# A hybrid decoder layer: attention's value products in float32r parts, heads in turn on two PSUM banks

## The chip, the cores and the metric

The kernel runs on one core of one Trainium2 chip. The metric is the device time of one execution in microseconds. TensorE (PE) multiplies matrices, VectorE (DVE) and ScalarE (ACT) work on rows of 128 partitions and also read PSUM, GpSimd (POOL) works in SBUF only, and SyncE (SP) issues the loads.

## The reference

One layer for 512 tokens of 1024 features, in float32. A normalised input goes through one projection; its columns feed three mixers, which are joined, projected by w_out and added to the input; a squared-ReLU MLP follows. The mixer that matters here is the sparse attention with 6 heads of 64 features on 2 key/value heads. For each head there are three softmaxes over keys: over 31 compressed blocks, over the selected blocks, and over a window. With 512 tokens the 16 selected blocks and the window of 512 hold every earlier key, so two of the three are plain causal attention with their own keys and values:

```python
p_c = masked_softmax(s, cmp_end[None, :] <= pos[:, None])
o_c = jnp.einsum('bhgqc,bhcd->bhgqd', p_c, vc)
...
o_s = jnp.einsum('bhgqn,bhqnd->bhgqd', masked_softmax(s, mask_s), vsel)
...
o_w = jnp.einsum('bhgqk,bhkd->bhgqd', masked_softmax(s, mask_w), vwb)
return gb[..., 0:1] * o_c + gb[..., 1:2] * o_s + gb[..., 2:3] * o_w
```

The other mixers are a gated delta rule (a chunked recurrence with 6 heads) and a causal pooling.

## The kernel before, in words

The kernel is written in a tile framework: the program gives instructions in an order, the framework puts each on its engine's queue by a schedule that it works out beforehand, and each queue then runs in order. A PSUM bank or a buffer of a pool is handed on in the order of the program; who asks for it waits until the last reader of the holder before is done.

Most large products are done in float32r parts: a value is cast to a high part (ACT) and the difference is the low part (DVE or GpSimd), and `mm3` (L142) issues high x high, high x low and low x high. `split_rows` (L147) makes both parts from PSUM. Some products stay in float32, which PE issues as two records each.

Up to about 252 us the input projection runs in slabs. Of these `vcopy` (L683) copies the attention's values for the four token blocks into `Vt`, `prep_heads` (L526) makes the queries and keys `XT`, and `compress_half` (L583) makes the compressed keys `KCT` and values `VC`. Beside them the delta rule's solves and its scan (`gdn_step`, L868) run on banks of their own; the scan's products use bank 3 (`ps_`), and after its nine steps `gdn_out` (L913) normalises each token block and transposes it through bank 3 (`go`) into chunks 0 to 2 of `yTh` and `yTl`.

The attention stage is `attentions` (L1140), walked in turn with `out_gdn` (L1210) by `side_by_side` (L936). Heads go in pairs. For each pair a bank 7 is taken as accumulator (`pa`), and for each of two branches and each head of the pair:

- `probs` (L1092): for each block i of 128 queries the scores against (i + 1) x 128 keys (L1100, L1101, float32r, and the mask L1102), their maximum (DVE), the exponential with its sum (ACT), and the scaling by gate over sum, blocks 0 to 2 on DVE and block 3 on ACT (L1113, L1115).
- `values` (L1117): the ten blocks of 128x128 probabilities are transposed in three groups (`BLKS`): four blocks with key block 0, three with key block 1 and one with key block 3, two with key block 2. Each group is copied from PSUM (first and third on ACT, second on DVE) and multiplied in float32 with 64 columns of values (L1135), the first head of a pair into rows 0 to 63 of the accumulator, the second into rows 64 to 127. The groups have 512, 384 + 128, and 256 columns.

The compressed branch (`cmp_probs`, L1056) gives transposed probabilities of three heads at once, and L1155 multiplies 32 rows of them per head with `VC`. `finish` (L1162) splits the pair's accumulator into one chunk of `yTh` and `yTl` (chunks 3 to 5).

`out_gdn` loads w_out by chunks of 128 rows (`load_w`, L1173: raw load on SP, high part on ACT, low part on DVE) into ten slots in two pools, and adds y times w_out to the residual in three passes (`out_tile`, L1196): chunks 6 and 7, then 0 to 2, and after the attention 3 to 5. The norm and the MLP follow.

Of the kernel before, what the change touches and what calls it, by code (L numbers as in the profile page):

```python
# [26 lines left out]
H = 6  # L27
# [10 lines left out]
def trunk_kernel(ctx, tc, x, norm_mix, w_in, conv_w, a_log, dt_bias, gdn_norm, nsa_q_norm, nsa_k_norm,  # L38
# [14 lines left out]
    def nm(s):  # L53
        _n[0] += 1
        return f"{s}{_n[0]}"
# [19 lines left out]


    r2 = ctx.enter_context(pool("r2", 1))
    N2 = 25

    def t2(shape, name, dt=F32):  # L80
        return r2.tile(shape, dt, tag="t", name=nm(name), bufs=N2)
# [308 lines left out]
    halves = [slice(0, 64), slice(64, 128)]  # L390

    XT, Vt = {}, {}
    VC = ctile([96, 2, HD], F32, "VC")
    KCT = ctile([P, 2, 64], F32R, "KCT")
    kr = gdp.tile([P, NT, H, HD], F32, tag="kr", name="kr")
    qr = gdp.tile([P, NT, H, HD], F32, tag="qr", name="qr")
# [186 lines left out]
    def compress_half(a, q):  # L583
        if q == 0:
            cst_[a] = pc_(), flat[a]
        acc, fs = cst_[a]
        for j in range(8 * q, 8 * q + 8):
            r0 = P * j
            with tc.issue_after(slabs2.ins):
                hi, lo = load_half([(0, cmp_w1[0, a, r0:r0 + P, :])], "c", (4, 2, 1), "AV")  # L590
            for n_, w in enumerate((hi, lo)):
                PE.matmul(acc[:, 0:256], fs[j // 4][:, j % 4, :], w[:, 0, :], start=(j == 0 and n_ == 0),  # L592
                          stop=(j == 15 and n_ == 1))
            yield 0.21
        if q == 0:
            return
        w2 = cmp_.tile([P, 2, HD], F32, tag="w2", name=nm("w2"))
        S.dma_start(w2, cmp_w2[0, a].rearrange("(m p) d -> p m d", p=P))
        hid = cmp_.tile([P, 256], F32, tag="hid", name=nm("hid"))
        S.copy(hid, acc[:, 0:256])  # L600
        hp_ = acc[:, 256:384]
        for m in range(2):
            PE.matmul(hp_[:, ts(m, 64)], hid[:, ts(m, P)], id2, start=True, stop=True)
        hh = cmp_.tile([P, 128], F32, tag="hh", name=nm("hh"))
        ht = cmp_.tile([P, 128], F32, tag="ht", name=nm("ht"))
        S.activation(ht, hp_[:, 0:128], AF.Tanh, scale=0.5)
        S.mul(hh, hp_[:, 0:128], 0.5)
        V.scalar_tensor_tensor(hh, ht, 1.0, hh, ALU.add, ALU.mult)
        if a == 0:
            kp = acc[:, 384:448]  # L610
            for m in range(2):
                PE.matmul(kp[0:64, 0:HD], hh[:, ts(m, 64)], w2[:, m, :], start=(m == 0), stop=(m == 1))
            kcs = cmp_.tile([64, HD], F32, tag="kcs", name=nm("kcs"))
            ss = sml.tile([P, 1], F32, tag="ss1", name=nm("ss"))
            r = sml.tile([P, 1], F32, tag="r1", name=nm("r"))
            S.activation(kcs, kp[0:64, 0:HD], AF.Square, accum_out=ss[0:64])
            V.tensor_scalar(ss[0:64], ss[0:64], 0.5 / HD, 0.5 * EPS, ALU.mult, ALU.add)
            rsqrt(r[0:64], ss[0:64], 1, 64)
            V.scalar_tensor_tensor(kcs, kp[0:64, 0:HD], r[0:64], gk_b[0:64, 0, :], ALU.mult, ALU.mult)
            kx = cmp_.tile([64, 2, P], F32, tag="hid", name=nm("kx"))  # L620
            S.copy(kx[:, 0, 0:HD].bitcast(F32R), kcs)
            S.copy(kx[:, 0, HD:P].bitcast(F32R), kcs)
            V.tensor_tensor(kx[:, 1, 0:HD], kcs, kx[:, 0, 0:HD], ALU.subtract)
            V.tensor_tensor(kx[:, 1, HD:P], kcs, kx[:, 0, 0:HD], ALU.subtract)
            kq = acc[:, 0:128]
            for b in range(2):
                PE.transpose(kq[:, ts(b, 64)], kx[:, b, :], ident[:64, :64])
            S.copy(KCT.rearrange("p k (b n) -> p b k n", b=2), kq[:, 0:128].rearrange("p (b k n) -> p b k n", b=2, k=2))
        else:
            vp = acc[:, 384:512]  # L630
            for rep in range(3):
                for kv in range(2):
                    for m in range(2):
                        PE.matmul(vp[32 * rep:32 * rep + 32, ts(kv, HD)], hh[:, 64 * m + 32 * kv:64 * m + 32 * kv + 32],
                                  w2[:, m, :], start=(m == 0), stop=(m == 1))
            S.copy(VC, vp[0:96, 0:128].rearrange("p (k d) -> p k d", k=2))


    PW = ctile([P, 2, P], F32, "PW")
# [41 lines left out]
                G.tensor_tensor(z3, z3, gnh.unsqueeze(1).to_broadcast([P, n // HD, HD]), ALU.mult)  # L681

    def vcopy(b0, pss):  # L683
        for b in range(2):
            if b not in Vt:
                Vt[b] = t2([P, 2, 4, HD], "Vt")
            S.copy(Vt[b][:, :, b0:b0 + 2, :], pss[b][:, :, 0:128].rearrange("p i (k d) -> p i k d", k=2))

    def conv_slab(cols):
        fs = {"q": 0, "k": 384, "v": 768, "u": 2718}  # L690
# [354 lines left out]
    wr = ctx.enter_context(pool("wr", 2, side="right"))  # L1045
    nwe = ExitStack()
    nw = nwe.enter_context(pool("nw", 2, side="right"))
    wop = [nwe.enter_context(pool(f"wo{n}", n, side="right")) for n in (4, 6)]
    gd.close()
    fe = ExitStack()  # L1050
    wq = fe.enter_context(pool("wq", 2))


    pn, pt_, pa = banks(0, 1), banks(2, 6), banks(7)

    def cmp_probs(kv):  # L1056

# [25 lines left out]
        tp = pt_()  # L1083
        for i in range(NT):
            PE.transpose(tp[0:96, ts(i, P)], pc[:, i].rearrange("p g n -> p (g n)"), ident)
        pt = nw.tile([96, T], F32, tag=f"pcT{kv}", bufs=1, name=nm("pcT"))
        S.copy(pt, tp[0:96])
        return pt

    BLKS = ([(0, i) for i in range(4)], [(1, i) for i in range(1, 4)] + [(3, 3)], [(2, 2), (2, 3)])  # L1090
# [1 line left out]
    def probs(h, br, out):  # L1092

        kv = h // 3
        kb = 6 + 4 * br + 2 * kv
        sm = sml.tile([P, NT], F32, tag="sm4", bufs=4, name=nm("sm"))
        for i in range(NT):
            n = (i + 1) * P
            sc = pn()
            PE.matmul(sc[:, 0:n], XT[h][:, ts(i, P)], XT[kb][:, 0:n], start=True, stop=False)  # L1100
            PE.matmul(sc[:, 0:n], XT[h][:, ts(i, P)], XT[kb + 1][:, 0:n], start=False, stop=False)  # L1101
            PE.matmul(sc[:, n - P:n], identb, negb, start=False, stop=True)  # L1102
            mx = sml.tile([P, 1], F32, tag="mx", bufs=4, name=nm("mx"))
            V.tensor_reduce(mx, sc[:, 0:n], AX.X, ALU.max, negate=True)
            p_ = nw.tile([P, n], F32, tag=f"P{i}", name=nm("P"))
            S.activation(p_, sc[:, 0:n], AF.Exp, bias=mx, accum_out=sm[:, i:i + 1])
            out.append(p_)
            yield 0.11 * (i + 1)
        V.reciprocal(sm, sm)
        V.tensor_tensor(sm, sm, gate[:, :, 3 * h + 1 + br], ALU.mult)  # L1110
        for i in range(NT):
            if i == 3:
                S.mul(out[i], out[i], sm[:, i:i + 1])  # L1113
            else:
                V.tensor_scalar(out[i], out[i], sm[:, i:i + 1], None, ALU.mult)  # L1115

    def values(acc, h, br, Ps):  # L1117

        a = h % 2
        for b, blks in enumerate(BLKS):  # L1120
            n = len(blks) * P
            tp = pt_()
            for c, (k, i) in enumerate(blks):
                PE.transpose(tp[:, ts(c, P)], Ps[i][:, ts(k, P)], ident)  # L1124
            pt = nw.tile([P, n], F32, tag=f"pt{b}", name=nm("pt"))
            if b == 1:
                V.tensor_copy(pt, tp[:, :n])
            else:
                S.copy(pt, tp[:, :n])
            yield 0.4  # L1130
            c = 0
            while c < len(blks):
                k, i = blks[c]
                m = sum(1 for x_ in blks if x_[0] == k)
                PE.matmul(acc[halves[a], i * P:(i + m) * P], Vt[k // 2][:, k % 2, 2 * br + h // 3, :],  # L1135
                          pt[:, c * P:(c + m) * P], start=False, stop=(br == 1 and k == 2), skip_group_check=True)
                c += m
            yield 0.4

    def attentions():  # L1140
        last = iter(())
        for pr in range(3):
            hd = (2 * pr, 2 * pr + 1)
            for h in hd:
                if h % 3 == 0:
                    pcT[h // 3] = cmp_probs(h // 3)
            acc = pa()
            for br in range(2):
                for h in hd:
                    Ps = []  # L1150
                    yield from in_turn((probs(h, br, Ps), last))
                    if br == 0 and h == hd[0]:
                        for a, h_ in enumerate(hd):
                            r = slice(32 * (h_ % 3), 32 * (h_ % 3) + 32)
                            PE.matmul(acc[halves[a]], VC[r, h_ // 3], pcT[h_ // 3][r], start=True, stop=False,  # L1155
                                      skip_group_check=True)
                    last = values(acc, h, br, Ps)
                    if br == 1 and h == hd[1]:
                        last = finish(last, pr, acc)
        yield from last  # L1160

    def finish(gen, pr, acc):  # L1162
        yield from gen
        y_tiles((3 + pr,))
        split_rows(yTh[3 + pr], yTl[3 + pr], acc)
        have.add(("y", 3 + pr))

    pcT = {}


    wo = {}
# [11 lines left out]

    def load_wo(*cs):
        for c in cs:
            wo[c] = load_w(wop[c < 4], w_out[0, ts(c, P), :].unsqueeze(1), "wo", "AV")

    w1s = []
    PASS = [(6,7),(0,1,2),(3,4,5)]
# [215 lines left out]
```

## Time and profile before

| | |
|---|---|
| median of three runs | 734.46 us (734.19 to 738.3) |
| the profiled execution | 738.01 us |
| its span, first to last instruction | 736.0 us |
| mean granted clock of TensorE | 0.986 |

The profile is one execution, taken with the hardware profiler. Its span is 2.0 us shorter than its time. An instruction's duration is not the time that it adds on PE: matmuls overlap, and the start of the next tells how long one holds the engine. The chain of waits is the chain of work that ended last, followed back, and its pieces add up without overlap.

### The profile page before, as it was taken

To read this page: it belongs to the slowest core of one execution; us is meant where nothing else is said; L and a number is where in the kernel's file an instruction comes from. 1 tells how busy PE (TensorE), PEld (TensorE's weight loads), DVE (VectorE), ACT (ScalarE), POOL (GpSimd) and SP (SyncE) were. 2 spreads that over 40 slices of the span, in tenths; PEclk is the share of its full clock that TensorE was granted. 3 is DMA by queue.
4 is the path that set the end of the run, shared out by engine and by line. 5 is a ranking of instruction groups with operands and counts; after the bars stand their busy time and mean duration, and the time that the engine had idled before them with its cause. 6 is when DMAs were issued, how large, how long until landed. Compare 5 with 4: busy or idle time off the path is not lost.

```text
span 736.0 us, 13221 instructions
## 1 busy us (share of the span) xinstructions
PE 707.9 (96%) x5147; PEld 566.7 (77%) x5147; DVE 550.3 (75%) x1010; ACT 369.6 (50%) x728; POOL 214.4 (29%) x292
## 2 busy tenths in 40 slices
PE   8999978999999899999999999999999999999997
PEld 6888766788889766665568987888888888888885
DVE  5776997688786596866545799796868587796836
ACT  5455834456673364555534745444553454445440
POOL 5734355350614410000010150504123050504123
PEclk9999988999999999999999999999999999999999
DMA  6243222124221251013002142514142332412103
GB/s 218 65 116 85 73 50 66 31 65 115 74 59 31 86 209 51 29 58 115 0 1 87 53 166 64 177 30 144 56 154 75 115 114 77 152 36 80 57 1 114
DMA packets 49779, 61.67 MB, mean 84 GB/s; under 512 B 5479, under 2 KB 42549, under 8 KB 49718
## 3 DMA queue, kind: packets, MB, share of 16 engines
q1 hardware_dynamic: 48852, 60.64, 26.2%
q8 instruction: 40, 0.66, 0.4%
q10 hardware_dynamic: 866, 0.20, 0.1%
q14 instruction: 21, 0.17, 0.1%
HBM read 58.73 MB, written 2.10 MB: 83 GB/s over the span
## 4 chain that ended last, share of the span: by engine, by line
PE 63%; DVE 7%; ACT 2%; issue 1%; DMA 0%; POOL 0%; ACTq 0%; DVEq 0%; POOLq 0%
PE ps L143 16%; PE ps L145 16%; PE ps L144 16%; PE ps L1135 4%; PE ps L429 3%; PE ps L1124 2%; PE ps L800 1%; PE ps L1100 1%; PE ps L1101 1%; PE ps L905 1%; DVE x L1374 1%; PE ps L592 1%; DVE bl L1281 1%; DMA raw<-in_w_out_dram 0%; PE ps L1247 0%
## 5 line engine op out<-in xcount | busy, mean ns | idle before, releaser
L145 PE MATMUL ps<-h2h,lw 128*128 128x512 f32 (+1 forms) x280 | 104.9, 376 | 0.0
L144 PE MATMUL ps<-h2l,hw 128*128 128x512 f32 (+1 forms) x280 | 104.4, 374 | 0.1
L143 PE MATMUL ps<-h2h,hw 128*128 128x512 f32 (+1 forms) x280 | 103.8, 374 | 0.0
L1288 POOL TENSOR_TENSOR al<-gF,ah 128x512 fp32r<-128x512 f32 x24 | 34.7, 1446 | 230.0 <-ACT ah L1287 191.0
L143 PE MATMUL ps<-bh,ah 128*128 128x512 f32 x224 | 88.5, 395 | 0.6 <-DVE x L1374 0.6
L144 PE MATMUL ps<-bl,ah 128*128 128x512 f32 x224 | 88.2, 394 | 0.0
L145 PE MATMUL ps<-bh,al 128*128 128x512 f32 x224 | 84.7, 394 | 0.0
L1374 DVE TENSOR_TENSOR x<-ps,x 128x512 f32<-128x512 f32 x112 | 73.0, 682 | 14.2 <-PE ps L145 14.1
L1281 DVE TENSOR_TENSOR bl<-w2r,bh 128x1024 fp32r<-128x1024 f32 x40 | 57.8, 1447 | 7.2 <-ACT bh L1280 7.2
L135 POOL TENSOR_TENSOR lo<-raw,hi 128x512 fp32r<-128x512 f32 (+1 forms) x36 | 48.1, 1351 | 50.2 <-ACT hi L134 50.0
L144 PEld LDWEIGHTS ps<-h2l,hw 128*128 128x128 f32 x280 | 52.6, 188 | 10.6 <-DVE h2l L1252 0.3
L145 PEld LDWEIGHTS ps<-h2h,lw 128*128 128x128 f32 x280 | 52.5, 188 | 10.0
L143 PEld LDWEIGHTS ps<-h2h,hw 128*128 128x128 f32 x280 | 52.3, 188 | 9.7
L1288 POOL TENSOR_TENSOR al<-gS,ah 128x512 fp32r<-128x512 f32 x32 | 54.0, 1705 | 17.3 <-ACT ah L1287 17.3
L1280 ACT CAST bh<-w2r 128x1024 fp32r<-128x1024 f32 x40 | 41.8, 1048 | 32.1 <-PE ps L145 31.9
L134 ACT CAST hi<-raw 128x512 fp32r<-128x512 f32 (+1 forms) x76 | 36.9, 517 | 33.2 <-DMA raw<-in_w_in_dram 14.5
L143 PEld LDWEIGHTS ps<-bh,ah 128*128 128x128 f32 x224 | 42.1, 188 | 11.2 <-ACT ah L1287 0.8
L145 PEld LDWEIGHTS ps<-bh,al 128*128 128x128 f32 x224 | 42.1, 188 | 9.9
L144 PEld LDWEIGHTS ps<-bl,ah 128*128 128x128 f32 x224 | 42.1, 188 | 9.7
L135 DVE TENSOR_TENSOR lw<-raw,hw 128x1024 fp32r<-128x1024 f32 x32 | 39.1, 1254 | 9.6 <-ACT hw L134 9.4
L134 ACT CAST hw<-raw 128x1024 fp32r<-128x1024 f32 x32 | 32.2, 1047 | 26.4 <-PE ps L144 23.4
L144 PE MATMUL ps<-hTl,hi 128*128 128x512 f32 x104 | 43.6, 420 | 0.0
(365 smaller groups left out, 1691.0 us busy)
## 6 DMA issues: line engine op xcount, KB each, us to landing
raw<-in_w_ffn_dram SPq DMA_DIRECT2D x32, 512.0 KB, 3.7
w2r<-in_w_ffn_dram SPq DMA_DIRECT2D x32, 512.0 KB, 4.5
raw<-in_w_in_dram SPq DMA_DIRECT2D x24, 256.0 KB, 2.8
raw<-in_w_in_dram SPq DMA_DIRECT2D x36, 128.0 KB, 2.4
x<-in_x_dram SPq DMA_DIRECT2D x8, 512.0 KB, 5.7
raw<-in_cmp_w_dram SPq DMA_DIRECT2D x32, 128.0 KB, 2.2
raw<-in_w_out_dram SPq DMA_DIRECT2D x8, 512.0 KB, 4.1
out_dram<-x SPq DMA_DIRECT2D x8, 256.0 KB, 2.0
```

The costliest lines, as they stand in the source:

```text
L134: {"A": S.copy, "V": V.tensor_copy, "G": G.tensor_copy}[e[0]](hi[:, k], r)
L135: {"V": V, "G": G}[e[1]].tensor_tensor(lo[:, k], r, f32v(hi[:, k]), ALU.subtract)
L143: PE.matmul(ps, ah, bh, start=start, stop=False, **kw)
L144: PE.matmul(ps, ah, bl, start=False, stop=False, **kw)
L145: PE.matmul(ps, al, bh, start=False, stop=stop, **kw)
L429: PE.matmul(ps[:, ts(i, 256)], a_[:, k, ts(2 * b + i, P)], w_, start=(k == 0 and n_ == 0 and i == 0), stop=(k == KC - 1 and n_ == 2 and i ...
L1124: PE.transpose(tp[:, ts(c, P)], Ps[i][:, ts(k, P)], ident)
L1135: PE.matmul(acc[halves[a], i * P:(i + m) * P], Vt[k // 2][:, k % 2, 2 * br + h // 3, :], pt[:, c * P:(c + m) * P], start=False, stop=(br = ...
L1280: S.copy(hi, src)
L1281: V.tensor_tensor(lo, src, f32v(hi), ALU.subtract)
L1288: G.tensor_tensor(lo, src, f32v(hi), ALU.subtract)
L1374: V.tensor_tensor(x2[i][:, cs], acc[bk, t_], x2[i][:, cs], ALU.add)
```

## The change

- The value tiles `Vt` are one per token block; for blocks 0, 1 and 3 they hold [high | low] float32r parts side by side, 128 columns. Block 2 stays float32.
- In `values` the first two groups' transposed probabilities become high and low float32r parts (a cast on ACT, a subtraction on DVE), and each is multiplied with the 128 columns, so rows 0 to 63 of the accumulator hold the products with high values and rows 64 to 127 those with low ones. The third group stays as it was and goes to rows 0 to 63, and its copy stays on ACT.
- One accumulator belongs to one head and not to a pair. Heads go one after the other, both branches of each, on banks 7 and 3 in turn.
- The compressed values become [high | low] parts, zero outside a head's 32 rows (`VCz`), the compressed probabilities high and low parts, and each head has two float32r matmuls.
- `finish` runs for each head: ACT copies the low-value rows, DVE adds the others, and after each second head the chunk is split as before.
- Block 2's probabilities are scaled on ACT, as block 3's are.
- w_out's low parts are computed on GpSimd. The pool of six w_out slots is opened after the delta rule's pools are closed, and the common pool has 27 buffers for 25.

```diff
-    N2 = 25
+    N2 = 27
...
-    VC = ctile([96, 2, HD], F32, "VC")
+    VC = ctile([96, 2, 2, HD], F32R, "VC")
...
-            S.copy(VC, vp[0:96, 0:128].rearrange("p (k d) -> p k d", k=2))
+            split_rows(VC[:, :, 0], VC[:, :, 1], vp[0:96, 0:128].rearrange("p (k d) -> p k d", k=2))
...
     def vcopy(b0, pss):
-        for b in range(2):
-            if b not in Vt:
-                Vt[b] = t2([P, 2, 4, HD], "Vt")
-            S.copy(Vt[b][:, :, b0:b0 + 2, :], pss[b][:, :, 0:128].rearrange("p i (k d) -> p i k d", k=2))
+        for i in range(NT):
+            src = pss[i // 2][:, i % 2, 0:128].rearrange("p (k d) -> p k d", k=2)
+            if i not in Vt:
+                Vt[i] = t2([P, 4, HD], "Vt") if i == 2 else t2([P, 4, 2, HD], "Vt", F32R)
+            if i == 2:
+                S.copy(Vt[i][:, b0:b0 + 2], src)
+            else:
+                split_rows(Vt[i][:, b0:b0 + 2, 0], Vt[i][:, b0:b0 + 2, 1], src)
...
-    wop = [nwe.enter_context(pool(f"wo{n}", n, side="right")) for n in (4, 6)]
+    wop = [nwe.enter_context(pool("wo4", 4, side="right"))]
     gd.close()
+    wop.append(nwe.enter_context(pool("wo6", 6, side="right")))
...
-    pn, pt_, pa = banks(0, 1), banks(2, 6), banks(7)
+    pn, pt_, pa = banks(0, 1), banks(2, 6), banks(7, 3)
...
-        pt = nw.tile([96, T], F32, tag=f"pcT{kv}", bufs=1, name=nm("pcT"))
-        S.copy(pt, tp[0:96])
+        pt = [nw.tile([96, T], F32R, tag=f"pcT{c}{kv}", bufs=1, name=nm("pcT")) for c in "hl"]
+        split_rows(pt[0], pt[1], tp[0:96])
...
-            if i == 3:
+            if i >= 2:
                 S.mul(out[i], out[i], sm[:, i:i + 1])
...
-            pt = nw.tile([P, n], F32, tag=f"pt{b}", name=nm("pt"))
-            if b == 1:
-                V.tensor_copy(pt, tp[:, :n])
+            if b == 2:
+                pt = [nw.tile([P, n], F32, tag=f"pt{b}", name=nm("pt"))]
+                S.copy(pt[0], tp[:, :n])
             else:
-                S.copy(pt, tp[:, :n])
+                pt = [nw.tile([P, n], F32R, tag=f"pt{c}{b}", name=nm("pt")) for c in "hl"]
+                split_rows(pt[0], pt[1], tp[:, :n])
...
-                PE.matmul(acc[halves[a], i * P:(i + m) * P], Vt[k // 2][:, k % 2, 2 * br + h // 3, :],
-                          pt[:, c * P:(c + m) * P], start=False, stop=(br == 1 and k == 2), skip_group_check=True)
+                for p_ in pt:
+                    v_ = Vt[k][:, 2 * br + h // 3]
+                    PE.matmul(acc[0:64 if b == 2 else P, i * P:(i + m) * P],
+                              v_ if b == 2 else v_.rearrange("p c d -> p (c d)"),
+                              p_[:, c * P:(c + m) * P], start=False, stop=(br == 1 and b == 2), skip_group_check=True)
...
     def attentions():
+        G.memset(f32v(VCz), 0.0)
+        for h in range(H):
+            r = slice(32 * (h % 3), 32 * (h % 3) + 32)
+            S.copy(VCz[r, h], f32v(VC[r, h // 3]).rearrange("p c d -> p (c d)"))
         last = iter(())
-        for pr in range(3):
-            hd = (2 * pr, 2 * pr + 1)
-            for h in hd:
-                if h % 3 == 0:
-                    pcT[h // 3] = cmp_probs(h // 3)
+        for h in range(H):
+            if h % 3 == 0:
+                pcT[h // 3] = cmp_probs(h // 3)
             acc = pa()
             for br in range(2):
-                for h in hd:
-                    Ps = []
-                    yield from in_turn((probs(h, br, Ps), last))
...
+                Ps = []
+                yield from in_turn((probs(h, br, Ps), last))
+                if br == 0:
+                    for n_, p_ in enumerate(pcT[h // 3]):
+                        PE.matmul(acc, VCz[:, h], p_, start=n_ == 0, stop=False, skip_group_check=True)
+                last = values(acc, h, br, Ps)
+            last = finish(last, h, acc)
         yield from last
...
-    def finish(gen, pr, acc):
+    def finish(gen, h, acc):
         yield from gen
...
+        a = halves[h % 2]
+        if h % 2 == 0:
+            os_[0] = nw.tile([P, T], F32, tag="o", bufs=1, name=nm("o"))
+        o = os_[0]
+        S.copy(o[a], acc[halves[1 - h % 2]])
+        V.tensor_tensor(o[a], acc[a], o[a], ALU.add)
+        if h % 2:
+            y_tiles((3 + h // 2,))
+            split_rows(yTh[3 + h // 2], yTl[3 + h // 2], o)
+            have.add(("y", 3 + h // 2))
...
-            wo[c] = load_w(wop[c < 4], w_out[0, ts(c, P), :].unsqueeze(1), "wo", "AV")
+            wo[c] = load_w(wop[c < 4], w_out[0, ts(c, P), :].unsqueeze(1), "wo", "AG")
```

## Rows read from the trace of the kernel before

**Rows 1.** The page: busy time, share of the span and instructions of each engine.

```profile
PE 707.9 (96%) x5147; PEld 566.7 (77%) x5147; DVE 550.3 (75%) x1010; ACT 369.6 (50%) x728; POOL 214.4 (29%) x292
```

**Rows 2.** Busy time of each engine in three stretches of the attention stage.

```profile
core 0: us, PE busy (x) PEld busy (x) DVE busy (x) ACT busy (x) POOL busy (x), PEclk, DMA share, GB/s
252.00:293.00 41.00, 39.77 (x344) 27.25 (x343) 33.48 (x86) 22.36 (x54) 6.54 (x8) 1.00 0.43 155
293.00:318.00 25.00, 23.97 (x125) 16.25 (x126) 19.08 (x63) 13.18 (x38) 1.19 (x1) 1.00 0.07 22
318.00:373.60 55.60, 53.95 (x264) 30.88 (x264) 33.53 (x80) 31.19 (x83) 0.00 (x0) 1.00 0.18 58
```

**Rows 3.** The chain of waits from 318 to 374 us, its shares by line.

```profile
by line: PE ps L1135 35.6%; PE ps L1124 14.6%; PE ps L1100 9.2%; PE ps L143 7.5%; PE ps L145 6.6%; PE ps L144 6.2%; PE ps L1101 5.9%; PE ps L1155 3.6%; PE ps L1102 2.6%; ACT pt L1129 2.1%; ACT P L1106 1.9%; DVE mx L1104 1.7%; DVE P L1115 1.
```

**Rows 4.** The chain, pieces of values in float32: start us, us, what.

```profile
288.36 0.58 PE ps L1135 x2
...
290.75 1.00 PE ps L1135 x2
...
324.06 1.00 PE ps L1155 x4
...
372.11 1.44 PE ps L1135 x6
```

**Rows 5.** The chain, pieces in float32r of 384, 512 and 128 columns.

```profile
290.50 0.18 PE ps L1101
...
318.23 0.23 PE ps L143
...
319.20 0.11 PE ps L1101
```

**Rows 6.** Groups of ACT by form: busy us, mean ns of one, idle before.

```profile
L1113 ACT ACTIVATE P<-P,sm 128x512 f32<-128x512 f32 x12 | 8.6, 720 | 4.1 <-DVE sm L1110 2.9 <-DVE P L1115 0.8 <-DVE rs L111 0.5
...
L1129 ACT COPY pt<-ps 128x512 f32<-128x512 f32 x12 | 7.0, 585 | 14.0 <-PE ps L1124 13.8
...
L1106 ACT ACTIVATE P<-ps,mx 128x384 f32<-128x384 f32 x12 | 7.0, 583 | 5.5 <-DVE mx L1104 5.3 <-PE ps L1124 0.2
```

**Rows 7.** Groups of DVE by form.

```profile
L135 DVE TENSOR_TENSOR lwo<-raw,hwo 128x1024 fp32r<-128x1024 f32 x8 | 9.9, 1237 | 1.0 <-ACT hwo L134 1.0
...
L1127 DVE COPY pt<-ps 128x512 f32<-128x512 f32 x12 | 8.2, 686 | 3.2 <-PE ps L1124 3.1
...
L1115 DVE TENSOR_SCALAR P<-P,sm 128x384 f32<-128x384 f32 x12 | 5.0, 415 | 0.0
```

**Rows 8.** Groups of POOL by form, low parts of 512 and 256 columns.

```profile
L135 POOL TENSOR_TENSOR lo<-raw,hi 128x512 fp32r<-128x512 f32 x32 | 44.0, 1393 | 41.4 <-ACT hi L134 41.2
...
L135 POOL TENSOR_TENSOR lo<-raw,hi 128x256 fp32r<-128x256 f32 x4 | 4.0, 1020 | 8.8 <-ACT hi L134 8.8
```

**Rows 9.** Timeline, DVE's L1110 alone and beside a POOL operation: start us, us.

```profile
297.73 0.16 DVE L1110 TENSOR_TENSOR sm<-sm,gate 128x4 f32<-128x4 f32 x1
...
306.20 1.19 POOL L924 TENSOR_TENSOR vb<-vb,zt 128x384 f32<-128x384 f32 x1 [25.32 <-DVE vb L923]
...
306.64 0.77 DVE L1110 TENSOR_TENSOR sm<-sm,gate 128x4 f32<-128x4 f32 x1
```

**Rows 10.** Timeline: a w_out cast, the scan's last product, the outputs through bank 3.

```profile
264.81 1.04 ACT L134 CAST hwo<-raw 128x1024 fp32r<-128x1024 f32 x1
...
292.44 0.51 PE L905 MATMUL ps<-vn,QK 64*64 64x64 f32 x6
...
295.05 0.55 PE L927 MATMUL ps<-ident,vb 128*128 128x128 f32 x3
...
318.47 0.28 DVE L149 TENSOR_TENSOR yTl<-ps,yTh 128x128 fp32r<-128x128 f32 x1
```

**Rows 11.** Timeline: the split of the last pair of heads.

```profile
373.59 0.59 ACT L148 CAST yTh<-ps 128x512 fp32r<-128x512 f32 x1 [1.07 <-PE ps L1135]
...
374.21 0.69 DVE L149 TENSOR_TENSOR yTl<-ps,yTh 128x512 fp32r<-128x512 f32 x1 [3.16 <-ACT yTh L148]
```

More of the change, by code (lines that the diff above doesn't have):

```diff
@@ L1117, in values @@
     def values(acc, h, br, Ps):
-        a = h % 2
         for b, blks in enumerate(BLKS):
@@ L1140, in attentions @@
     def attentions():
+        G.memset(f32v(VCz), 0.0)
+        for h in range(H):
+            r = slice(32 * (h % 3), 32 * (h % 3) + 32)
+            S.copy(VCz[r, h], f32v(VC[r, h // 3]).rearrange("p c d -> p (c d)"))
         last = iter(())
-        for pr in range(3):
-            hd = (2 * pr, 2 * pr + 1)
-            for h in hd:
-                if h % 3 == 0:
-                    pcT[h // 3] = cmp_probs(h // 3)
+        for h in range(H):
+            if h % 3 == 0:
+                pcT[h // 3] = cmp_probs(h // 3)
             acc = pa()
             for br in range(2):
-                for h in hd:
-                    Ps = []
-                    yield from in_turn((probs(h, br, Ps), last))
[L1152 to L1159, printed above, removed]
+                Ps = []
[5 more added lines that the diff above has]
+            last = finish(last, h, acc)
         yield from last
-    def finish(gen, pr, acc):
+    def finish(gen, h, acc):
         yield from gen
-        y_tiles((3 + pr,))
-        split_rows(yTh[3 + pr], yTl[3 + pr], acc)
-        have.add(("y", 3 + pr))
+        a = halves[h % 2]
[8 more added lines that the diff above has]
+            have.add(("y", 3 + h // 2))
+    os_ = {}
     pcT = {}
+    VCz = nw.tile([96, H, P], F32R, tag="VCz", bufs=1, name="VCz")
     wo = {}
```

## The prediction

> **What bounds the kernel now.** I read the page first: PE is busy for 96% of the span and the next engine, DVE, for 75% [rows 1]. That share is a mean over stages, so I went to the stage that the change touches. It runs from 252 us, where the first load of w_out is issued, to 373.6, where the last attention values end. The windows view cuts it in three [rows 2]: up to 293 the recurrent scan and its steps still run beside attention, up to 318 the scan's outputs are normalised and transposed, and from 318 on there is only attention and the output projection. In all three PE has work for about 96% of the time. In the first two DVE is at 82% and 76%; in the third DVE and ACT are at 60% and 56%.
>
> Modelled ends make a busy PE look fuller than it is, so the third view is the chain of waits from 318 to 374. Its shares by line [rows 3]: L1135, the product of probabilities and values, has 35.6%; the transposes L1124 14.6%; all PE lines together 91.8%. So the last stretch is bound by what PE has to issue, and the largest item is the float32 product that the change rewrites. In the first 50 us DVE is nearly as full, so a microsecond taken off PE is worth less there.
>
> **The change, part by part.**
>
> *Values on PE.* A chain piece is time on the path, without the overlap that an instruction's own duration contains. Per head and branch the first block group costs 1.00 us (512 columns, two records), the second and third together 1.44, so 2.44 [rows 4]. Other pieces are a little dearer (0.58 for the third group standing alone) and I keep the cheap one. After the change the first two groups are float32r. The prices stand in the score matmuls and the output projection, which are float32r with 128 output rows already: 0.23 us for 512 columns, 0.18 for 384, 0.11 for 128 [rows 5]. Each is issued twice, for the high and the low part of the probabilities: 2 x (0.23 + 0.18 + 0.11) = 1.04. The third group stays float32: 0.58 [rows 4]. Sum 1.62, saved 0.82, and over 12 head-branches 9.8 us.
>
> *Compressed values.* Before, two heads' matmuls lie on different quarters of the array, and four records together take 1.00 us [rows 4]; three pairs make 3.0. After: six heads, two float32r matmuls of 512 columns each, 12 x 0.23 = 2.8. Saved 0.2.
>
> *ScalarE.* Per head-branch it gains the cast of the second group, 0.585, and the scaling of 384 columns. The cast is priced as the copy of 512 columns that ACT does for the first group; the exponential over 384 columns takes 0.583 and the scaling of 512 takes 0.72 [rows 6], and I take 0.58 for the scaling. Times 12 that is 14.0 us. Each head's end adds a copy of 64x512, priced as the 128x512 one, 0.58, six times 3.5; the six copies into the padded compressed values are small (under 0.6 each, estimated at 0.3), 1.8. Sum 19.3 on 66.7 us in the stage [rows 2]: 75% of a stage of 115 us. In the last stretch alone, with 8 of 12 head-branches, it is 31.2 + 8 x 1.17 + 5 x 0.58 = 43.5 us of about 49 (55.6 less 8 x 0.82), 89%. That isn't over the edge, but every head-branch now passes PE, ACT, DVE, PE in series, where it could take ACT or DVE before. Bounds: nothing, if the other head's scores cover it; all 10 us, if ACT ends last. The chain's non-PE share of 8% is about 9 us over the stage; I let it grow by a quarter: +2.0.
>
> *VectorE.* Per head-branch it loses the 384 scaling (0.415) and a copy (0.686) [rows 7] and gains two subtractions of 512 columns from PSUM (0.69 each, as yTl in [rows 11]): +0.28, 3.3 in all. Head ends: 6 x 0.69 = 4.1; compressed probabilities: 2 x 0.69 = 1.4. The w_out low parts leave: 8 x 1.237 = 9.9 [rows 7]. Net -1.1, price 0. Without that last item it would be +8.8 on the engine that the chain meets most before 300.
>
> *GpSimd.* It takes the 8 low parts. No row of it has 1024 columns: 512 take 1.393 us and 256 take 1.020 [rows 8]. Continued at that slope 1024 would be 2.14, by proportion 2.79; I take 2.4, 19 us on an engine with 7.7 busy in 122 [rows 2]. Two of them come at the stage's start among the scan's own POOL steps, the rest where it is idle. A row speaks against this [rows 9]: at 306.64 a DVE multiplication of 4 columns took 0.77 us, where it takes 0.16 at 297.73. It ended at 307.41 and the POOL operation beside it at 307.39, so DVE stood until POOL was done. The Trainium skill, SBUF — State Buffer, section "SBUF: two separate sides", says that VectorE and GpSimd share a port pair as an exclusive lock, held for a whole instruction, against DVE instructions with two SBUF inputs or in a two-port mode; by that rule the trace agrees, and eight longer holders are added. The sum above has no relief from DVE in it; the rival C below prices the hold.
>
> *Bank 3.* Heads now accumulate in banks 7 and 3 in turn, and bank 3 belongs to the scan steps (the last of their matmuls starts at 292.44) and then to the scan outputs, whose last reader is the yTl subtraction that starts at 318.47 [rows 10]. The second head's first matmul would be due when the third head-branch gets to its values, at 290.75 [rows 4]. So it waits for up to 28 us. Queued behind it are that head's values, and its transposed parts fill two buffers per group; not behind it are both branches' scores and transposes of this head, the scores of the next, the rest of the (6,7) output tiles and the (0,1,2) tiles as their columns arrive. Scores are about 1.6 us of PE for a head-branch (2 x 1280 columns by [rows 5], estimated) and transposes 1.0 (14.6% of 55.6 over eight, [rows 3]), so four sets of scores and two of transposes are 8.4, and 120 output matmuls of 0.23, 28 us, are to be placed beside them. The compressed scores of the second key head come later in the new order, so the scan outputs should end sooner. Bounds 0 and 28 - 8.4 = 19.6, if no output tile fits; I take 0.5, since there is filler enough.
>
> *w_out's six slots.* They move into memory that the scan still holds: counted in tile sizes, about half of them fall on tiles that the scan reads until its last step at 292.44, where the first of these casts ran at 264.81 before. Their first use comes after 295, where the first scan output is transposed [rows 10]. With a cast of 1.04 and 2.4 on POOL the first is ready near 297, the third (one more load) near 304. Bounds 0 and 8; I take 0.4.
>
> *Values split where they are projected*: six subtractions of 128 columns on DVE, 0.28 each as in [rows 10], beside casts on ACT, before a bank is free for later matmuls. Bounds 0 and 1.7; 0.3. *The last head* ends with a copy and an addition more, 1.3 us, before the 0.59 and 0.69 of chunk 5's yTh and yTl [rows 11]; the projection has three banks and works on chunks 3 and 4 meanwhile: bounds 0 and 1.3; 0.3.
>
> **Sum.** -9.8 - 0.2 + 2.0 + 0.5 + 0.4 + 0.3 + 0.3 = -6.5 us. The profiled execution took 738.01 us with a span of 736.0; it becomes 731.5. It lies 3.55 above the median of the three runs, 734.46, inside their spread; with the same difference the median becomes 728.0.
>
> **Rivals.** A measurement of this kernel tells about 1%, 7.3 us, from no change.
>
> A. The forecast: PE saves 10 and gives a third back; 724 to 731. For it: the 91.8% of the chain on PE. Chance 0.53, of which 0.29 below 727.1.
>
> B. More comes off: DVE loses the w_out low parts in its fullest stretch, 252 to 293 with 82% [rows 2], and the scan ends sooner. With 5 of the 9.9 us on the path the result is -11.5, 723, and no chain of the trace rules it out. Against it: POOL's low part is later than DVE's by 1.2. Chance 0.13.
>
> C. Another engine takes over: ACT at 89%, or DVE held by POOL. If all eight low parts hold a DVE instruction on the path for half their time, 8 x 1.2 = 9.6 us take the place of what PE saved: 734. For it the 0.77 row; against it that most DVE work here reads PSUM, and that the scheduling spreads the eight over 100 us. Chance 0.15, of which 0.02 slower.
>
> D. Slower: bank 3 holds the second head. PE's queue is in order; if the accumulating matmul stands in it before the filler, or the filler ends early because the (0,1,2) tiles wait for their weights and the same scan outputs, PE idles in 295 to 318. Of the 19.6 us that were its bound I give two and a half to output tiles: -10 + 17 + 1 (the three small terms) = +8, 742. It decides from 9 us of idle on. For it: the 28 us between the rows; against it the filler named above. Chance 0.19, of which 0.16 slower.
>
> **How the numbers follow.** Faster by over 1%: 0.29 + 0.13 = 0.42. Slower by over 1%: 0.02 + 0.16 = 0.18. Within: 0.40. A alone spans 724 to 731. With C, most of B and part of D the range is 719 to 740: below lies about half of B's tail, above what D costs at its worst.
>
> **What would show it.** Right: L1135's successor has pieces of 0.23 us and its share of the chain falls from 35.6% to about 25%; the stage from 252 ends 6 to 8 us earlier; ACT has about 86 us in it and POOL about 27. Wrong: the second head's compressed matmul waits on a yTl subtraction with PE idle (D); multiplications of 4 columns beside POOL's low parts take 2 us (C); PE waits for "pt" casts in the last stretch more than for its own queue (C by ACT). If the values' pieces of 128 columns cost far over 0.11, the main term was mis-sized.

## The result and the profile after

The changed kernel takes 742.44 us (median of 7 runs, 740.07 to 746.58) where the kernel before takes 737.82 in the same comparison: ratio 1.0068, 95% interval 1.0043 to 1.0093, some 5 us slower. The forecast was 728.0 with 719 to 740, so the sign was wrong and the time lies past the upper end. The kernel before gave medians of 736.8 to 738.0 in all later comparisons, not the 734.46 of the three runs shown, so everything below goes by ratios; 0.001 is 0.74 us.

The profiled execution took 746.58 us, the longest of its 7, so it shows the places better than the sizes. The engines' busy shares on its page are much as before [rows 1], but the chain isn't; these are the busy line, then the chain by engine in the changed kernel and in the kernel before:

```profile
PE 705.4 (95%) x5147; PEld 577.9 (78%) x5147; DVE 563.3 (76%) x1017; ACT 385.5 (52%) x768; POOL 237.7 (32%) x301
...
PE 47%; DVE 17%; ACT 4%; issue 3%; DMA 2%; POOL 1%; SPq 0%; DVEq 0%; ACTq 0%; POOLq 0%
...
PE 63%; DVE 7%; ACT 2%; issue 1%; DMA 0%; POOL 0%; ACTq 0%; DVEq 0%; POOLq 0%
```

The stage shows where. This is the windows view of the changed kernel, first the three stretches of [rows 2], then pieces of the first and the worst part of the second:

```profile
252.00:293.00 41.00, 39.83 (x366) 31.46 (x365) 31.39 (x86) 22.73 (x61) 10.35 (x10) 0.92 0.29 104
293.00:318.00 25.00, 17.12 (x90) 13.41 (x88) 21.45 (x49) 17.79 (x45) 10.41 (x5) 0.80 0.21 64
318.00:373.60 55.60, 51.14 (x278) 37.79 (x278) 41.98 (x92) 38.32 (x95) 5.79 (x2) 1.00 0.24 77
...
255.00:257.00 2.00, 1.10 (x16) 0.81 (x15) 2.00 (x8) 0.83 (x2) 0.74 (x2) 0.95 1.03 406
257.00:263.00 6.00, 5.97 (x57) 5.08 (x58) 5.01 (x11) 3.34 (x9) 5.78 (x5) 0.50 0.92 354
...
296.00:298.00 2.00, 1.73 (x9) 1.20 (x9) 2.00 (x8) 2.00 (x6) 0.99 (x1) 0.94 0.00 0
298.00:300.00 2.00, 0.14 (x2) 0.00 (x0) 2.00 (x3) 1.65 (x4) 2.00 (x2) 0.50 0.03 8
300.00:302.00 2.00, 0.18 (x1) 0.18 (x1) 2.00 (x3) 0.71 (x2) 1.68 (x1) 0.50 0.71 211
302.00:308.00 6.00, 6.00 (x24) 4.91 (x24) 3.93 (x20) 3.90 (x10) 1.00 (x1) 0.50 0.33 104
```

Between 293 and 318 us TensorE is busy for 17.1 of 25 us, where it was 24.0 before. From 298 to 302 it does next to nothing. Its granted clock is 0.50 (1.2 GHz, for 1.00 at 2.4 GHz) from 297.8, just ahead of this wait, to 308; before it fell TensorE had waited 1.16 us at 294.9. So the long wait didn't bring the fall, but the 6 us of full work behind it ran at half speed, some 3 us lost (estimated) beside 4 us of idleness. Half the clock is seen in the first stretch too, from 257 to 263, where TensorE had two waits under 0.5 us each. The profile of e8 below, a faster kernel, shows that as well and e5's doesn't, so it doesn't tell the changed kernel from the others. The last values start 7.3 us later than before. Both kernels' values, by line, with first and last start:

```profile
L1135 PE MATMUL ps<-pt,Vt x96: 272/458/644, 272.9 to 373.2; 128*64 128x512 f32 x24, 128*64 128x384 f32 x24, 128*64 128x128 f32 x24, 128*64 128x256 f32 x24
```

```profile
L1144 PE MATMUL ps<-pt,Vt x96: 221/379/505, 272.0 to 380.5; 128*128 128x512 f32 x24, 128*128 128x384 f32 x24, 128*128 128x128 f32 x24, 128*64 128x256 f32 x24
```

Two things empty the second stretch. The first is seen in three timelines of the changed kernel, GpSimd's, VectorE's and TensorE's:

```profile
297.01 4.67 POOL L135 TENSOR_TENSOR lwo<-raw,hwo 128x1024 fp32r<-128x1024 f32 x2 [17.93 <-ACT hwo L134]
...
308.18 2.38 POOL L135 TENSOR_TENSOR lwo<-raw,hwo 128x1024 fp32r<-128x1024 f32 x1 [1.61 <-ACT hwo L134]
```

```profile
297.02 0.42 DVE L1109 TENSOR_REDUCE mx<-ps 128x1 f32<-128x256 f32 x1
297.36 2.04 DVE L1115 TENSOR_TENSOR sm<-sm,gate 128x4 f32<-128x4 f32 x1
299.31 0.16 DVE L104 TENSOR_SCALAR r<-r 128x6 int32<-128x6 int32 x1
299.43 2.60 DVE L1120 TENSOR_SCALAR P<-P,sm 128x128 f32<-128x128 f32 x2
...
308.54 2.17 DVE L1120 TENSOR_SCALAR P<-P,sm 128x256 f32<-128x256 f32 x1
```

```profile
301.82 0.95 PE L1130 MATMUL ps<-ident,P 128*128 128x128 f32 x3 [3.68 <-DVE P L1120]
...
311.89 0.50 PE L145 MATMUL ps<-hwo,yTl 128*128 128x512 f32 x1 [1.98 <-DVE yTl L149]
```

A multiplication of 4 columns (0.16 us in [rows 9]) takes 2.04 and ends when the first low part ends; the first of the two scalings behind it ends with the second, at about 301.7; 0.1 us later the transposes that waited 3.68 us for it start. At 308 it happens again: the scaling holds back a yTl subtraction, and TensorE waits 1.98 for that. In the chain of waits of the stage six of the eight low parts have a held VectorE piece:

```profile
261.73 2.29 DVE sm L1085
...
297.44 1.95 DVE sm L1115
...
299.47 2.30 DVE P L1120
...
308.62 2.08 DVE P L1120
...
315.91 2.27 DVE P L1120 x2
...
323.08 1.97 DVE sm L1084
```

They are 12.9 us, where the same instructions would take some 1.7 (estimated from e5's forms). Against that VectorE is rid of 10 us of low parts. The forms view prices it over the whole stage; these are VectorE's scalings in the changed kernel and in the experiment e5 below, where no low part is on GpSimd:

```profile
L1120 DVE TENSOR_SCALAR P<-P,sm 128x128 f32<-128x128 f32 x12 | 7.3, 607 | 0.3
...
L1084 DVE TENSOR_TENSOR sm<-sm,gate 128x12 f32<-128x12 f32 x2 | 2.7, 1326 | 0.1
```

```profile
L1120 DVE TENSOR_SCALAR P<-P,sm 128x128 f32<-128x128 f32 x12 | 3.4, 283 | 0.2
...
L1084 DVE TENSOR_TENSOR sm<-sm,gate 128x12 f32<-128x12 f32 x2 | 0.4, 176 | 0.1
```

These two lines alone are 3.9 and 2.3 us longer. The maximum at 297.02, which reads PSUM, keeps its time beside the same low part.

The second is bank 3. TensorE's timeline around the stretch, compressed values (L1165) and values (L1144):

```profile
291.11 0.65 PE L1144 MATMUL ps<-pt,Vt 128*64 128x256 f32 x2
293.93 0.71 PE L1165 MATMUL ps<-pcT,VCz 96*128 96x512 f32 x2
...
330.17 0.71 PE L1165 MATMUL ps<-pcT,VCz 96*128 96x512 f32 x2
330.71 3.50 PE L1144 MATMUL ps<-pt,Vt 128*128 128x512 f32 x16
```

No value product runs from 291.8 to 330.7. The pair at 293.93 is the third head's, on the bank 7 that the first head had left; the second head, on bank 3, waits for the last reader of the scan's outputs, and the values of the third stand behind it. Then 16 records, two head-branches, run in one go. Values that might have filled TensorE's waits stood behind it, though e2 below shows that freeing them alone doesn't help. The last reader itself came later than before; VectorE's timelines, before and after:

```profile
320.02 0.28 DVE L149 TENSOR_TENSOR yTl<-ps,yTh 128x128 fp32r<-128x128 f32 x1
```

```profile
327.59 0.29 DVE L149 TENSOR_TENSOR yTl<-ps,yTh 128x128 fp32r<-128x128 f32 x1 [0.33 <-ACT yTh L148]
```

### The profile page after: what moved, and what is told of

It is laid out like the page before. It is cut to its first block, busy times and chain, and to the rows that moved or that the text cites. A ratio compares the mean times of both kernels' runs of the same rounds, so it can differ in the third digit from the quotient of the medians.

```text
span 744.6 us, 13266 instructions
## 1 busy us (share of the span) xinstructions
PE 705.4 (95%) x5147; PEld 577.9 (78%) x5147; DVE 563.3 (76%) x1017; ACT 385.5 (52%) x768; POOL 237.7 (32%) x301
## 4 chain that ended last, share of the span: by engine, by line
PE 47%; DVE 17%; ACT 4%; issue 3%; DMA 2%; POOL 1%; SPq 0%; DVEq 0%; ACTq 0%; POOLq 0%
PE ps L143 12%; PE ps L145 12%; PE ps L144 12%; PE ps L1144 2%; DVE bl L1298 2%; PE ps L429 2%; DVE lw L135 2%; PE ps L1130 2%; DVE x L1391 2%; DMA w2r<-in_w_ffn_dram 1%; DVE P L1120 1%; PE ps L909 1%; PE ps L1105 1%; DVE gS L1371 1%; DVE w2r L1328 1%
## 5 line engine op out<-in xcount | busy, mean ns | idle before, releaser
L1305 POOL TENSOR_TENSOR al<-gF,ah 128x512 fp32r<-128x512 f32 x24 | 38.7, 1611 | 217.3 <-ACT ah L1304 178.0
L143 PEld LDWEIGHTS ps<-bh,ah 128*128 128x128 f32 x224 | 42.1, 188 | 12.9 <-ACT bh L1297 1.6
L1304 ACT CAST ah<-gS 128x512 fp32r<-128x512 f32 x32 | 19.7, 620 | 53.8 <-DVE gS L1373 24.4
L135 DVE TENSOR_TENSOR lw<-raw,hw 128x1024 fp32r<-128x1024 f32 x32 | 42.3, 1355 | 4.1 <-ACT hw L134 4.1
```

The source lines that it names most:

```text
L135: {"V": V, "G": G}[e[1]].tensor_tensor(lo[:, k], r, f32v(hi[:, k]), ALU.subtract)
L143: PE.matmul(ps, ah, bh, start=start, stop=False, **kw)
L1304: S.copy(hi, src)
L1305: G.tensor_tensor(lo, src, f32v(hi), ALU.subtract)
```

## The experiments

Theory L: GpSimd's low parts hold VectorE. Theory B: bank 3 holds the second head. Theory S, added later: the late slots of w_out bunch its loads and low parts. The changed kernel, e1 to e4, e5 to e8, e9 to e12 and e13 to e16 were measured in five separate comparisons, each with the kernel before in it; a price taken across two of them is a difference of ratios, and e5 was measured in one of them only. These are all sixteen runs with their ratios to the kernel before:

| run | kernel | ratio | 95% interval |
|---|---|---|---|
| e1 | changed, low parts on VectorE | 1.0010 | 0.9994 to 1.0026 |
| e2 | changed, bank 7 for the first two heads | 1.0110 | 1.0091 to 1.0130 |
| e3 | before, low parts on GpSimd | 1.0032 | 1.0014 to 1.0050 |
| e4 | e1 and e2 together | 0.9972 | 0.9948 to 0.9995 |
| e5 | e4 and early slots for chunk 0 | 0.9944 | 0.9924 to 0.9963 |
| e6 | changed, low parts in quarters | 1.0024 | 1.0007 to 1.0042 |
| e7 | before, late slots | 0.9998 | 0.9978 to 1.0018 |
| e8 | e5, block 2 scaled on VectorE | 0.9941 | 0.9919 to 0.9962 |
| e9 | e5, no matmuls with P's low part | 0.9859 | 0.9832 to 0.9885 |
| e10 | e9, no low part of P at all | 0.9842 | 0.9816 to 0.9868 |
| e11 | e5, low parts on GpSimd in quarters | 0.9986 | 0.9965 to 1.0007 |
| e12 | e5, low parts on GpSimd | 1.0044 | 1.0025 to 1.0064 |
| e13 | e5, idle GpSimd subtractions added | 1.0111 | 1.0083 to 1.0139 |
| e14 | e5, banks 7 and 3 by turns | 1.0021 | 0.9997 to 1.0045 |
| e15 | e5, chunks 6 and 7 on GpSimd | 1.0004 | 0.9981 to 1.0027 |
| e16 | e5, chunks 0 to 2 on GpSimd | 1.0013 | 0.9989 to 1.0036 |

**The two suspects, one by one and together (e1 to e4).** The first edit is e1, the second e2, both are e4, and the reverse of the first in the kernel before is e3.

```diff
-wo[c] = load_w(wop[c < 4], w_out[0, ts(c, P), :].unsqueeze(1), "wo", "AG")
+wo[c] = load_w(wop[c < 4], w_out[0, ts(c, P), :].unsqueeze(1), "wo", "AV")
...
-pn, pt_, pa = banks(0, 1), banks(2, 6), banks(7, 3)
+pn, pt_, pa = banks(0, 1), banks(2, 6), banks(7, 7, 3, 7, 3, 7)
```

Expected of e1: 

> The changed kernel with w_out's low parts back on VectorE, nothing else undone. Theory L (a GpSimd low part of 2.5 us holds VectorE's small multiplications and scalings, so PE waits behind them): the six VectorE instructions that took 2.0 to 2.6 us take 0.2 to 0.6 again, PE's wait of 3.7 us for the scaled probabilities is gone, and the ratio to the kernel before falls from 1.007 to 0.993 to 0.999. Theory B (the second head waits for bank 3 until 328 us, and that alone costs the time): the ratio stays at 1.004 to 1.009.

Expected of e2: 

> The changed kernel with the heads on banks 7, 7, 3, 7, 3, 7 in place of 7 and 3 in turn, so that the second head doesn't wait for the scan outputs. Theory B: the second head's compressed matmuls start near 294 in place of 330 us, PE's busy time in 293 to 318 rises from 17 of 25 to 22 or more, and the ratio falls to 0.996 to 1.001. Theory L: the order changes, but PE still waits behind VectorE, and the ratio stays at 1.003 to 1.009.

Expected of e3: 

> The kernel before with w_out's low parts on GpSimd, nothing else. Theory L: VectorE is held here too, up to 8 times 2 us less the 9.9 us that it no longer spends itself; the ratio is 1.003 to 1.010. Theory B, and any theory that puts the cost into the new accumulators or the later weights: 0.997 to 1.002.

Expected of e4: 

> The changed kernel with both edits: low parts on VectorE and banks 7, 7, 3, 7, 3, 7. If L and B both hold and add: 0.985 to 0.993, the saving on PE's values shows at last. If only L holds: as with the low parts on VectorE alone, within 0.002. If only B holds: as with the banks alone, within 0.002. If neither, 1.003 to 1.009.

Moving the low parts back takes 0.0058 off, 4.3 us; the same move costs the kernel before 2.4 us (e3). Theory L holds, though e1 fell short of the ratio that it expected, 0.993 to 0.999. The bank edit alone was a miss: not better and perhaps worse. In its trace the second head's finish has moved into the held stretch, and here even the split's yTl subtraction, which reads SBUF twice, is held (0.69 us in the changed kernel); VectorE's timeline:

```profile
297.05 2.60 DVE L1120 TENSOR_SCALAR P<-P,sm 128x128 f32<-128x128 f32 x2
...
314.87 2.83 DVE L149 TENSOR_TENSOR yTl<-o,yTh 128x512 fp32r<-128x512 f32 x1
```

Behind it TensorE does nothing from 316 to 318, and its clock is at 0.50 from 320 to 322. With the hold gone (e4 against e1) the same edit takes 2.8 us off, so B is a cost, but not by itself. e4 stays short of the 0.985 to 0.993 that it expected of both theories together; why e2 came out above the changed kernel is not settled beyond these rows.

**Slots, pieces and ScalarE (e5 to e8).** e5 opens `wo2` (2 slots, chunks 0 and 3) before the scan's pools close and `wo4b` (4 slots, chunks 1 and 2) after; e7 puts the changed kernel's order of pools into the kernel before; e8 is `if i == 3` for `if i >= 2` in the scaling; e6 is

```diff
...
+for q_ in range(4):
+    G.tensor_tensor(lo[:, k, ts(q_, 256)], r[:, :, ts(q_, 256)], f32v(hi[:, k, ts(q_, 256)]), ALU.subtract)
```

Expected of e5: 

> The kernel with both earlier edits (low parts on VectorE, bank 7 twice in turn) plus two slots for w_out chunk 0 that are there before the gated delta part closes, as in the kernel before; nothing is left out. Theory S (late slots bunch the raw loads, casts and low parts of w_out between 286 and 305 us, where they run as one serial chain through two raw buffers): the first cast stands near 265 us again, the chain of that stretch is gone, ratio to before 0.988 to 0.994. Rival (the slots are hidden, VectorE and ScalarE bound the stretch anyway): 0.995 to 0.999, as without the edit.

Expected of e6: 

> The changed kernel with each w_out low part cut into four GpSimd subtractions of 256 columns; same work otherwise. Theory L1 (a VectorE instruction that meets a GpSimd subtraction waits for the end of that one instruction): the held multiplications of 4 columns and reciprocals take under 0.9 us instead of 2.0 to 2.6, and the ratio to before falls from 1.007 to 1.001 to 1.004. Rival L2 (the loss comes from the total time that GpSimd is busy, or from work that waits for the low parts themselves): the ratio stays at 1.005 to 1.010, since GpSimd's total grows slightly.

Expected of e7: 

> The kernel before with one edit: the pool of six w_out slots is opened only after the gated delta part has closed, as in the changed kernel. Nothing is left out. Theory S: the late loads alone cost part of what is missing, ratio 1.002 to 1.006, with the w_out casts bunched after 286 us. Rival (hidden, as the prediction's +0.4 us has it): 0.9990 to 1.0015.

Expected of e8: 

> The kernel of e5_early_slots with the scaling of block 2 back on VectorE; same work otherwise. If ScalarE is what the stage waits for, as the prediction's +2.0 us for ScalarE has it: 0.002 to 0.004 below e5 in ratio. If VectorE is the fuller engine of the stage: 0.001 to 0.004 above it. If neither: within 0.001.

The slots cost the kernel before nothing (e7). In the repaired kernel early ones may be worth 2.1 us (e5 against e4), but the two intervals overlap, and e14 below, which is e1 with early slots, is no better than e1. e8 equals e5: where block 2 is scaled makes no difference. Quarters on GpSimd take 3.2 us off the changed kernel although GpSimd's own time grows from 19.9 to 22.8 us. What shrinks is the hold; GpSimd's and VectorE's forms in e6:

```profile
L137 POOL TENSOR_TENSOR lwo<-raw,hwo 128x256 fp32r<-128x256 f32 x32 | 22.8, 744 | 41.7 <-ACT hwo L134 41.6
```

```profile
L1124 DVE TENSOR_SCALAR P<-P,sm 128x128 f32<-128x128 f32 x12 | 4.4, 367 | 0.3
...
L1088 DVE TENSOR_TENSOR sm<-sm,gate 128x12 f32<-128x12 f32 x2 | 0.6, 292 | 0.1
```

The same two lines as above are at 367 and 292 ns, where the changed kernel has 607 and 1326. A hold that ends with one instruction, and not a shared rate, does this. Low parts that come late to TensorE don't explain the gain either: four quarters take 3.0 us, one whole low part 2.5.

**What bounds the repaired kernel (e9, e10).** `for p_ in pt[:1]` leaves the low part's matmuls out; e10 drops its subtraction too.

Expected of e9: 

> e5_early_slots without the values' matmuls of the low part of P (36 matmuls, 12 x 1024 columns, about 12 x 0.45 = 5.4 us of TensorE); VectorE still makes the low parts. Leaves out the low part of P in the two large groups. Theory P (TensorE is the bound of the stage throughout): 5 to 6 us less than e5, ratio to before 0.986 to 0.988. Rival V (the chain goes through VectorE and ScalarE for much of the stage, so that TensorE's saving comes off in part only): 0 to 3 us less, ratio 0.990 to 0.9945.

Expected of e10: 

> e9_no_low_matmul without the low parts themselves: VectorE's 24 subtractions of 0.60 us for P are gone too (14.4 us). Leaves out the low part of P in the two large groups, as e9 does. Theory P: no more than 1 us below e9. Rival V: 3 to 8 us below e9, ratio to before 0.980 to 0.988.

e9 takes 0.0085 off e5, 6.3 us. The matmuls left out are 12 x (0.23 + 0.18 + 0.11) = 6.2 us by [rows 5]; the expectation had counted 5.4. So TensorE's time comes off in full, as far as the intervals tell. Leaving out VectorE's 14.4 us as well (e10) changes the ratio by 0.0017, inside both intervals. The stage is still TensorE's, once nothing holds VectorE.

**The hold again, from the repaired side (e11 to e16).** e11 and e12 are the edits of e6 and of the changed kernel in e5; e14 is `banks(7, 3)`; e15 and e16 are `"AG" if c > 5` and `"AG" if c < 3`; e13 is

```diff
...
+if tag == "wo":
+    G.tensor_tensor(scr.tile([P, 1, 1024], F32, tag="s", name=nm("scr")), r, f32v(hi[:, k]), ALU.subtract)
```

Expected of e11: 

> e5_early_slots with the w_out low parts on GpSimd again, each as four subtractions of 256 columns; same work otherwise. If VectorE is what e5 waits for, its 8 x 1.13 = 9 us come off it and the held instructions cost at most 0.6 us each: ratio 0.990 to 0.994. If the hold costs as much as it frees: 0.994 to 0.999.

Expected of e12: 

> e5_early_slots with the w_out low parts on GpSimd whole, as in the changed kernel: that kernel with bank 7 twice and two early slots. Theory E (the place decides: low parts that bunch beside the gated delta's output cost more than spread ones): 2 us over e5 as in e3_before_low_on_pool, ratio 0.996 to 0.998. Rival (the hold costs the same wherever the low parts stand): 4 us or more over e5, as the changed kernel stands over e1_low_on_dve, ratio 0.999 to 1.002.

Expected of e13: 

> e5_early_slots (low parts on VectorE) plus, for each of the eight w_out chunks, a GpSimd subtraction of the same two operands into a scratch tile that nobody reads. Theory H (the hold itself costs: VectorE's instructions wait for GpSimd's to end): 4 to 8 us over e5, ratio to before 1.000 to 1.005. Rival (the cost lay in low parts that came late to TensorE): within 1.5 us of e5, ratio 0.992 to 0.9965.

Expected of e14: 

> e5_early_slots with the banks of the accumulators as in the changed kernel (7 and 3 by turns, so the second head takes bank 3). Theory B2 (bank 3 is held by the gated delta's output, and the second head waits for it): 2 to 4 us over e5, ratio 0.997 to 1.000. The prediction's price of 0.5 us: 0.994 to 0.996.

Expected of e15: 

> e5_early_slots with the low parts of chunks 6 and 7 alone on GpSimd (they run near 254 us, ahead of the attention's values). If the place decides (they meet VectorE where TensorE has other work): within 1.5 us of e5, ratio 0.993 to 0.9965. If each low part costs the same, a quarter of e12's 7.4 us: 0.996 to 0.998; both answers are near, so the trace (TensorE's waits and granted clock at 250 to 262 us) is read beside it.

Expected of e16: 

> e5_early_slots with the low parts of chunks 0, 1 and 2 alone on GpSimd (chunk 0 near 263 us, 1 and 2 near 292 us beside the gated delta's output). If the place decides: most of e12's 7.4 us, 4 to 7 us over e5, ratio 0.999 to 1.004. If each low part costs the same, three eighths of it, 2.8 us: 0.997 to 0.9995.

GpSimd whole costs e5 7.4 us, in quarters 3.1. The expectation for e12 that a better place would make it cheap was a miss, and its rival's range was passed too: it costs more here than in the changed kernel, perhaps because there a blocked head hid a part. Two chunks cost 4.4 us (above both expectations of e15), three 5.1, all eight 7.4: neither place alone decides, and the parts don't add up. In e16 the wait of TensorE is the one already seen:

```profile
PE ps L1130 <- DVE P L1120: 3.6, 1, 3.6
```

e13 leaves VectorE its low parts and lets GpSimd subtract for nobody: 12.3 us, where 4 to 8 were expected. No low part comes from GpSimd there, so late ones can't be what it pays for; that leaves the hold, but the size isn't clean. Now VectorE's own low part is held (3.38 us for 1.24), VectorE has all its work besides, and the idle subtraction keeps the raw buffer, so the loads of w_out are issued until 340 us, in e5 until 304.

e14 gives bank 3 its price on e5, a kernel with no such hold: 5.7 us, where 2 to 4 were expected. TensorE's timeline and its windows in e14, and below them the same windows in e5:

```profile
321.35 0.63 PE L1165 MATMUL ps<-pcT,VCz 96*128 96x512 f32 x2
321.82 3.50 PE L1144 MATMUL ps<-pt,Vt 128*128 128x512 f32 x16
```

```profile
300.00:304.00 4.00, 2.77 (x12) 1.95 (x11) 3.63 (x7) 2.90 (x8) 0.99 (x1) 0.70 0.03 8
304.00:308.00 4.00, 4.00 (x15) 3.62 (x16) 1.87 (x9) 2.56 (x6) 0.00 (x0) 0.50 0.36 123
308.00:312.00 4.00, 4.00 (x16) 3.37 (x15) 3.97 (x12) 1.10 (x4) 0.00 (x0) 0.52 0.41 122
```

```profile
300.00:304.00 4.00, 3.66 (x19) 2.19 (x18) 3.93 (x8) 3.77 (x10) 1.02 (x1) 1.00 0.00 0
304.00:308.00 4.00, 3.61 (x25) 2.77 (x23) 3.47 (x9) 3.69 (x8) 0.00 (x0) 1.00 0.39 131
308.00:312.00 4.00, 3.03 (x17) 2.06 (x16) 4.00 (x12) 1.69 (x5) 0.00 (x0) 1.00 0.28 84
```

In e14 TensorE waits 1.23 us after 300, the clock falls to 0.50 at 301.6 and stays there to about 312; in e5 value products fill the place (TensorE's timeline) and the clock stays at 1.00:

```profile
300.39 0.94 PE L1144 MATMUL ps<-pt,Vt 128*128 128x512 f32 x3
301.86 0.61 PE L1144 MATMUL ps<-pt,Vt 128*128 128x384 f32 x3 [0.30 <-DVE pt L149]
```

The repaired kernels, e5 (733.1 us, 0.9944 of before) and e8 with one edit less (732.7, 0.9941), are some 0.6% faster than the kernel before, with intervals that leave 1 out.

## Why the prediction was wrong

**Right: the main term.** It put a head-branch of values at 1.62 us. The chain of the changed kernel shows two of them without a gap:

```profile
330.88 3.34 PE ps L1144 x16
```

That is 1.67 each. L1144's share of the chain from 318 to 381 us is 21.9%, where 35.6% was to fall to about 25%. e9 shows that such time comes off, and e5 is faster than before by 0.0056, 4.1 us.

**The step that failed first: "Net -1.1, price 0", with GpSimd's low parts at 2.4 us "on an engine with 7.7 busy in 122".** The low part takes 2.50 us, so the duration was right. Its effect on VectorE had a row of its own [rows 9] and the rule beside it, and still stood only in rival C, as an alternative to the forecast and not as a term of the sum. Measured, with what VectorE saves already taken off, it is 4.3 us (changed kernel to e1) and 7.4 on the repaired one, where the sum has 0. C's 9.6 us of hold is near what the chain shows, 12.9 less some 1.7, and its sign, multiplications of 4 columns at 2 us, is there. C's argument against itself, "that most DVE work here reads PSUM", is only just true (53 of 98 us in the stage before, by the forms view) and beside the point: the instructions on SBUF stand in the one queue ahead of those on PSUM, and each transposition needs one of them. The Trainium skill, SBUF — State Buffer, "SBUF: two separate sides", has the shared ports as a lock held for a whole instruction; by that rule the traces agree, with 2.04 for 0.16 us, and with the smaller loss in quarters.

**The second: "Bank 3 ... I take 0.5, since there is filler enough".** The wait was seen (28 us forecast, 39 without a value product in the profile after) but the filler wasn't enough: TensorE had 17.1 us of work in 25. The sum moved only scores and output tiles into the gap and left to rival D that output tiles themselves wait, for yTl from VectorE and for w_out. Two readings under it were wrong as well: the last reader in the kernel before starts at 320.02, not at 318.47, and the scan's outputs, which "should end sooner", ended 7.6 us later. Measured: 2.8 us (e1 to e4) to 5.7 (e5 to e14). This is rival D's mechanism at a sixth to a third of its price of 17, and that D's sum came to 742, which was measured, is luck: the hold of VectorE isn't in it. The row that D named as its sign, the head waiting with TensorE idle, showed as TensorE waiting for VectorE, since the head's products were simply not in the queue yet.

**A term that was missing: the granted clock.** All three stretches of [rows 2] stood at 1.00, and the forecast took it for given. In the changed kernel TensorE worked for some 6 us at 0.50 in the first stretch and again from 302 to 308, in e14 for some 10 in the second. No run separates what this costs from the waits around it.

**Slots, 0.4.** Nothing in the kernel before (e7), perhaps 2.1 in the repaired one; not told apart.

**ScalarE, +2.0.** The scaling part of it is not seen (e8). After all repairs the sum without bank 3 and slots, -6.5 - 0.9 = -7.4, still promises 3.3 us more than the -4.1 of e5 (-5.6 to -2.7 by its interval), which has w_out's low parts back on VectorE. A part of that may be what TensorE waits for the two parts of P in e5, by the waits view, against 0.3 for copies before; no run separates it:

```profile
PE ps L1144 <- DVE pt L149: 2.0, 5, 0.7
...
PE ps L1144 <- ACT pt L148: 0.8, 2, 0.5
```

From the changed kernel to e5 the three repairs together are worth 0.0124, 9.1 us; their prices measured one by one around e5 (7.4, 5.7 and 2.1) add up to 15. So they overlap. That each fills the same stretch, some 15 us from 294 on, is how the traces read; no run shows it.

## What to carry to other kernels

An operation moved to GpSimd isn't priced by GpSimd's idle time: price it by the VectorE instructions on SBUF that run beside it, each held for up to the whole duration of the operation, and by who waits behind them in VectorE's queue; take off what VectorE no longer does. When a head or tile is given a bank that another stage still holds, count what TensorE can still run until then, without the work that depends on the busy engine. Two waits that each look covered can use up the same cover.

## What the runs showed of the hardware

A GpSimd subtraction of 128x1024 (2.3 to 2.5 us) held VectorE instructions of 3 to 12 columns, which take 0.16 to 0.18 us, so that they took up to 2.36 (e12), a scaling with one SBUF tensor as well as products of two, and in e13 a VectorE subtraction of 128x1024 took 3.38 us; four subtractions of 256 columns took 0.74 us each and held less. It goes the other way too: in e13 a GpSimd subtraction that started 0.1 us after VectorE's of 128x1024 took 3.36 us. The granted clock fell to 0.50 in the changed kernel at 297.8, after a wait of 1.16 us, and in e14 at 301.6, after one of 1.23; in both it was back at 1.00 some 10 us later. In the first stretch it fell at 256.8, between waits of 0.48 and 0.44 us, where e5 had waits of 0.49 and 0.44 us at the same place and stayed at 1.00.
